# First-stage reordering in a two-layer diffusion trunk: raw products of four FFN column blocks, with the shift added later as a bias

## Chip, cores, metric

One Trainium2 chip, all 8 cores, every core running the same program on its own tokens. The metric is the device time in microseconds of the slowest core. "us" is microseconds throughout. Engines go by their names in the trace: PE is TensorE (matmuls), DVE VectorE, ACT ScalarE, POOL GpSimd, SP SyncE; PSUM is the memory into which PE writes its products (`ps` in the trace). Some executions are in a slower state: cores of one die (cores 0 to 3 or 4 to 7), or pairs of cores, show a lower granted TensorE clock (in one execution of head_only cores 0 to 3 had 0.811 to 0.819 and took 1687 to 1696 us, in another cores 2 to 5 had 0.968 to 0.971 and took 1455 to 1459; the other cores had 0.988 or more and took 1427 to 1432). Only fast executions enter the ratios. I also use "undisturbed cores": the mean span of all cores whose mean granted clock was 0.988 or more, over all executions of a kernel. That mean is steadier than a median.

## The reference, cut to what matters

```python
D_MODEL, D_FF, DEPTH = 1024, 2816, 2
def modulate(x, g, shift, scale):
    return rms_norm(x, g) * (1 + scale[:, None, :]) + shift[:, None, :]
def swiglu(h, w1, w2):
    gate, up = jnp.split(h @ w1, 2, axis=-1)
    return (jax.nn.silu(gate) * up) @ w2
# each layer: FFN 1, mixer, FFN 2; layer 0's mixer is convolution + attention, layer 1's pools
mod = jax.nn.silu(cvec) @ ada_w[l] + ada_b[l]            # 9 vectors of 1024 per layer
sh1, sc1, g1, sh2, sc2, g2, sh3, sc3, g3 = jnp.split(mod, 9, axis=-1)
x = x + 0.5 * g1 * swiglu(modulate(x, norm_g[l, 0], sh1, sc1), ffn_w1[l, 0], ffn_w2[l, 0])
# ... mixer with sh2, sc2, g2; second FFN with sh3, sc3, g3
```

The change uses a plain identity: with `r` the norm factor, `(x*r*scale + shift) @ W = (x*r*scale) @ W + shift @ W`. The second product does not depend on the token, so it is a bias per column.

## The kernel before

Tokens are split into three tiles per core: 512, 512 and 256 columns (`TILES`), held transposed, eight chunks of 128 features each. Operations are yielded by generators, and a scheduler places them on the engines in time order of a model, so the diff alone doesn't tell the final order. The first up-projection has 22 column blocks (`w1`), each 1 MB read as fp32 and stored as 512 KB of bf16. A modulation slot (`ada`) is as big: slots 0 to 3 of layer 0 hold the first shift, 4 to 7 the first scale; these eight are done on PE ("16 matmuls of 128x2" in the trace), all later ones as vector dots on DVE ("CUSTOM_DVE" in the trace, 4 per slot). All weights arrive through one queue of loads and one ring of 16 buffers:

```python
def seq():                                   # the order of loads
    a = list(w1(0, 0))
    for i in range(4):
        if i == 3:
            yield from a[0:2]
        yield from ada(0, 4 + i, 5 + i)      # scale
        yield from ada(0, i, i + 1)          # shift
    yield from a[2:6]
    self.pace = 0                            # from here loads are spaced by LOAD_GAPS
    yield from mix(a[6:], ada(0, 8, 24))
    yield from w2(0, 0)
    yield from ada(0, 24, 28)
    # ... mixer weights ...
    yield from mix(w1(0, 1), list(ada(0, 28, 36)) + list(ada(1, 0, 0)))
    yield from w2(0, 1)
    yield from ada(1, 0, 17)
    # ... layer 1 ...
yield from self.xtile(0, POOL)               # tile 0; tiles 1 and 2 are put in between:
for key, src, shape in seq():
    if key in (("ada", 0, 6), ("w1", 0, 0, 3)):
        yield from self.xtile(1 if key[0] == "ada" else 2, POOL)

def xload(self):                             # small tables and two row broadcasts, on another queue
    yield self.wait(("w", ("ada", 0, 3)))    # ... only after this slot has landed
    self.late = self.W[("ada", 0, 3)][1]
```

The norm of a tile makes squares by a plan (which engine squares each chunk, and whether PE sums it alone or it is first added up), then scales on DVE and adds the shift, mostly on ACT:

```python
A8 = [(ACT, False)] * 8                              # squares on ACT, added up on DVE
P8 = [(POOL, False)] * 6 + [(ACT, False)] * 2        # six squares on POOL, added up on POOL
Q8 = [(POOL, False)] * 6 + [(ACT, True)] * 2         # the two of ACT summed on PE
IN = [(ACT, True), (DVE, True)] * 4                  # every square summed on PE, in fp32
norms(1, 0, 0, [IN, IN, A8])                         # first FFN's norm, tiles 0, 1, 2
norms(2, 0, 1, [P8, P8, Q8], sh=(ACT, ACT, DVE))     # the norm before mixer 0
# in norm():
for c in range(8):
    yield self.wait(("mod", l, i, c // 2), 2)        # scale AND shift of this chunk
    yield self.stt(nv, xres[c], asc[c], r, ALU.mult, ALU.mult, ...)      # DVE
    # then hbuf = nv + shift, on ACT
```

## Time and profile before

Three runs took 1430.21 to 1431.3 us, median 1430.92. The profiled execution was a slow one, and its second die shows why it is not read:

The spans and clocks of the cores, kernel before (two of its lines):

```profile
core 0: 1427.0 us, clock 0.992
...
die 1 (median of its cores): 1442.5 us, clock 0.981
```

So I read core 0, of the undisturbed die. The table of stretches for it (stretch in us, then busy us and count of PE, weight loads, DVE, ACT, POOL; then the granted clock, the busy share of the DMA engines, and GB/s moved):

```profile
20.00:40.00 20.00, 11.41 (x80) 5.34 (x80) 6.67 (x15) 6.57 (x11) 2.84 (x6) 0.74 1.03 223
40.00:60.00 20.00, 15.15 (x76) 5.74 (x77) 9.21 (x17) 9.43 (x14) 1.10 (x3) 0.75 1.00 194
60.00:80.00 20.00, 20.00 (x94) 9.20 (x93) 9.29 (x18) 15.40 (x24) 0.00 (x0) 1.00 1.03 181
80.00:100.00 20.00, 20.00 (x128) 12.39 (x127) 16.00 (x30) 7.22 (x16) 0.53 (x1) 1.00 0.73 124
...
400.00:500.00 100.00, 96.53 (x1127) 50.73 (x1126) 55.16 (x135) 92.97 (x105) 20.56 (x23) 1.00 0.46 79
```

PE is full from about 57 us on, apart from small holes in the mixer and in attention. Before that it starves, while the DMA share is 1.0. The timeline of PE shows for what (start, duration, instruction and count; in brackets the idle time before it and what ended it; `sb_hbuf,sb_ring` is FFN work, `sb_scb` modulation, `sb_onesf` the sums of the norm):

```profile
22.52 0.58 PE L309 MATMUL ps<-sb_scb,sb_ring 128*128 128x2 bf16 x16 [3.22 <-DMA sb_ring<-adaw]
25.37 0.59 PE L309 MATMUL ps<-sb_scb,sb_ring 128*128 128x2 bf16 x16 [2.27 <-DMA sb_ring<-adaw]
28.82 8.52 PE L309 MATMUL ps<-sb_sq,sb_onesf 128*128 128x512 f32 x14 [2.86 <-ACT sb_sq L325]
...
45.40 6.70 PE L309 MATMUL ps<-sb_hbuf,sb_ring 128*128 128x512 bf16 x20 [1.24 <-ACT sb_hbuf L325]
...
56.71 14.78 PE L309 MATMUL ps<-sb_hbuf,sb_ring 128*128 128x512 bf16 x60 [1.68 <-ACT sb_hbuf L325]
```

A useful number for such a head is the *effective dense start*: the time at which PE would have had to start, without a pause, to be where it is. The first FFN's up-projection is 704 matmuls of 512 columns and 352 of 256, at the dense pace 704 x 0.2157 + 352 x 0.1092 = 190.3 us; it ended at 241.4 us, so this start is 51.1 us.

### The profile page before, as it was taken

What the parts mean: (1) busy time and instruction counts of PE and PEld (TensorE: products, weight loads), DVE (VectorE), ACT (ScalarE), POOL (GpSimd) and SP (SyncE); (2) the same over time, 40 slices, a digit from 0 to 9 for tenths busy, and PEclk for the clock granted to TensorE, in tenths of its full rate; (3) what the DMA queues carried; (4) which work ended last, traced back from release to release, by engine and by line L of the source; (5) the groups of instructions that cost most, each with busy time, mean ns of one, the idle gap of its engine ahead of it and who ended that gap; (6) DMA issues with size and microseconds to landing.
All of it is one profiled execution on the core that took longest, in us unless ns stands there. A gap on an engine that the chain in (4) does not pass through costs nothing.

```text
span 1443.6 us, 21515 instructions; the slowest of 8 cores (1423.7 to 1443.6 us)
## 1 busy us (share of the span) xinstructions
PE 1409.3 (98%) x8742; PEld 768.4 (53%) x8742; DVE 842.0 (58%) x1505; ACT 494.8 (34%) x824; POOL 207.1 (14%) x308
## 2 busy tenths in 40 slices
PE   5899999999999999999999999999999999999998
PEld 2355555457644554655544655555446646555446
DVE  2468872866656596342599977773575862222245
ACT  3441111035589956211123331111134771111112
POOL 3001111843312200110010011111110000000000
PEclk8899999999999999999999999999999999999999
DMA  9967779322555423663463377777861255550012
GB/s 201 190 110 123 125 121 172 70 34 39 93 90 88 75 39 65 101 118 59 74 105 58 58 122 127 121 125 119 131 106 30 44 88 89 94 95 16 0 59 89
DMA packets 42435, 132.24 MB, mean 92 GB/s; under 512 B 6240, under 2 KB 10080, under 8 KB 42336
## 3 DMA queue, kind: packets, MB, share of 16 engines
q0 software_dynamic: 34816, 122.52, 50.1%
q1 hardware_dynamic: 7520, 8.34, 1.8%
q8 instruction: 69, 1.13, 0.3%
q14 instruction: 30, 0.25, 0.1%
HBM read 241.55 MB, written 6.55 MB: 172 GB/s over the span
## 4 chain that ended last, share of the span: by engine, by line
PE 92%; POOL 2%; DVE 2%; ACT 2%; DMA 2%; issue 1%; DVEq 0%; ACTq 0%; POOLq 0%
PE ps L309 91%; DMA sb_xres<-xin 2%; DVE sb_nt L330 1%; POOL sb_ring L335 1%; POOL sb_sq L335 1%; ACT sb_sg L325 0%; POOL sb_acc L335 0%; POOL sb_areg L1306 0%; ACT sb_hbuf L325 0%; PE ps L318 0%; DVE sb_xres L330 0%; ACT sb_areg L325 0%; DVE sb_sq L688 0%; DVE sb_areg L330 0%; DVE sb_areg L335 0%
## 5 line engine op out<-in xcount | busy, mean ns | idle before, releaser
L309 PE MATMUL ps<-sb_hbuf,sb_ring 128*128 128x512 bf16 (+1 forms) x4512 | 842.9, 347 | 6.8 <-ACT sb_hbuf L325 3.6
L309 PEld LDWEIGHTS ps<-sb_hbuf,sb_ring 128*128 128x128 bf16 x4512 | 439.1, 99 | 380.4 <-issue 36.0
L309 PE MATMUL ps<-sb_areg,sb_ring 128*128 128x512 bf16 (+2 forms) x2480 | 428.0, 334 | 0.6 <-DVE sb_xres L330 0.6
L335 DVE TENSOR_TENSOR sb_areg<-ps,sb_sg 128x512 bf16<-128x512 f32 (+1 forms) x264 | 157.9, 602 | 327.6 <-PE ps L309 301.0
L325 ACT ACTIVATE sb_sg<-ps 128x512 f32<-128x512 f32 (+3 forms) x279 | 145.9, 527 | 544.5 <-PE ps L309 520.2
L309 PEld LDWEIGHTS ps<-sb_areg,sb_ring 128*128 128x128 bf16 x2480 | 229.3, 99 | 193.8 <-issue 19.7
L688 DVE CUSTOM_DVE_ANT_0 sb_sq<-sb_ring,sb_crow,sb_adab 128x1024 bf16<-128x1024 bf16 x128 | 167.4, 1308 | 22.7 <-DMA sb_ring<-adaw 22.1
L688 DVE CUSTOM_DVE_ANT_0 sb_ring<-sb_ring,sb_crow,sb_adab 128x1024 bf16<-128x1024 bf16 x128 | 167.6, 1309 | 2.4
L325 ACT ACTIVATE sb_sq<-sb_xres 128x512 f32<-128x512 f32 (+2 forms) x133 | 70.1, 534 | 267.4 <-DVE sb_xres L330 186.2
L330 DVE SCALAR_TENSOR_TENSOR sb_xres<-ps,sb_gsc,sb_xres 128x512 f32<-128x512 f32 (+2 forms) x160 | 98.3, 628 | 88.4 <-PE ps L309 87.4
L360 POOL DMA_DIRECT2D sb_ring<-w1t x88 | 47.2, 537 | 462.9 <-PE ps L309 397.9
L330 DVE SCALAR_TENSOR_TENSOR sb_nt<-sb_xres,sb_asc,sb_acc 128x512 f32<-128x512 f32 (+1 forms) x144 | 90.5, 664 | 12.8 <-ACT sb_acc L325 8.4
L325 ACT ACTIVATE sb_hbuf<-sb_nt,sb_modsb 128x512 bf16<-128x512 f32 (+1 forms) x136 | 84.9, 656 | 37.5 <-DVE sb_nt L330 37.1
L335 DVE TENSOR_TENSOR sb_acc<-sb_acc,sb_sq 128x512 f32<-128x512 f32 (+2 forms) x119 | 68.3, 574 | 26.6 <-ACT sb_sq L325 25.1
L360 POOL DMA_DIRECT2D sb_ring<-adaw x72 | 38.5, 539 | 302.9 <-PE ps L309 186.7
L325 ACT ACTIVATE sb_sg<-ps,sb_amask 128x1024 bf16<-128x1024 f32 x63 | 68.1, 1119 | 5.2 <-PE ps L309 4.9
L309 PE MATMUL ps<-sb_areg 128*128 128x65 bf16 (+3 forms) x600 | 61.1, 266 | 2.1 <-ACT sb_sg L325 1.8
L360 POOL DMA_DIRECT2D sb_ring<-w2t x44 | 23.3, 531 | 188.7 <-PE ps L309 175.0
L309 PEld LDWEIGHTS ps<-sb_areg 128*128 128x128 bf16 (+1 forms) x600 | 28.9, 96 | 38.1 <-issue 27.3
L309 PE MATMUL ps<-sb_ring,sb_hbuf 128*128 128x256 bf16 x320 | 38.1, 274 | 0.6 <-ACT sb_areg L325 0.3
L309 PE MATMUL ps<-sb_sq,sb_onesf 128*128 128x512 f32 (+2 forms) x44 | 24.2, 685 | 14.6 <-DVE sb_sq L335 11.0
L325 ACT ACTIVATE sb_areg<-ps,sb_amask 128x1024 bf16<-128x1024 f32 x33 | 36.3, 1116 | 4.0 <-PE ps L309 3.7
(74 smaller groups left out, 486.0 us busy)
## 6 DMA issues: line engine op xcount, KB each, us to landing
sb_ring<-w1t POOLq DMA_DIRECT2D x88, 512.0 KB, 5.1
sb_ring<-adaw POOLq DMA_DIRECT2D x72, 512.0 KB, 5.6
sb_ring<-w2t POOLq DMA_DIRECT2D x44, 512.0 KB, 5.2
sb_xres<-xin POOLq DMA_DIRECT2D x4, 1024.0 KB, 17.1
yo<-sb_xres SPq DMA_DIRECT2D x8, 512.0 KB, 3.0
sb_areg<-mp POOLq DMA_DIRECT2D x5, 512.0 KB, 8.2
sb_ring<-wcx POOLq DMA_DIRECT2D x4, 512.0 KB, 13.3
sb_ring<-wo POOLq DMA_DIRECT2D x4, 512.0 KB, 11.4
```

The costliest lines, as they stand in the source:

```text
L309: ins = e.matmul(m[0], lhsT=m[1], rhs=m[2], start=m[3], stop=m[4], **({"skip_group_check": True} if len(m) > 5 else {}))
L325: o = Op(ACT, lambda e: e.activation(out=out, in_=in_, func=func, **kw), reads, writes, cost)
L330: return Op(DVE, lambda e: e.scalar_tensor_tensor(out=out, in0=in0, scalar=scalar, in1=in1, op0=op0, op1=op1), reads, writes, 150.0 + 1.04 ...
L335: return Op(eng, lambda e: e.tensor_tensor(out=out, in0=in0, in1=in1, op=op), reads, writes, c)
L360: return Op(q, lambda e: e.dma_start(out=out, in_=in_), reads, writes, 600.0 if q == POOL else 450.0, True, nbytes, key)
L688: return Op(DVE, lambda e: e.tensor_tensor_reduce(out=prod, in0=w, in1=self.crow[:, v, :], scale=1.0, scalar=bias, op0=ALU.mult, op1=ALU.a ...
```

## The change

Intent: the last shift lands much later than the last scale could. So the four scale slots and four `w1` blocks are loaded before the four shift slots, and PE multiplies the scaled tokens of tiles 0 and 1 with those four blocks while the shifts are still on their way. The products are put aside in fp32 on chip. Later `shift @ W` is made for the four blocks (one column of PE output each), and the silu and the product take it as a bias. Three side changes come with it: the plans of the first norm (tile 1, the second tile, from `IN` to `A8`; tile 2, the third, from `A8` to `Q8`), the shift-adds of every other chunk of the second tile, which go from ACT to POOL, and a retuning of the gaps and the order of later loads and vector dots.

```diff
-ADA_GAP0, ADA_GAP = 600.0, 600.0
-LOAD_GAPS = (3900.0, 4400.0, 4000.0, 5500.0)
+ADA_GAPS = (((0, 22), 1000.0), ((0, 28), 600.0), ((0, 32), 600.0), ((1, 4), 1500.0), ((1, 13), 900.0), ((1, 26), 1500.0), ((1, 36), 800.0))
+NRAW = 4
+LOAD_GAPS = (3700.0, 4200.0, 4100.0, 5500.0)
 ... in seq():
-            for i in range(4):
-                if i == 3:
-                    yield from a[0:2]
-                yield from ada(0, 4 + i, 5 + i)
-                yield from ada(0, i, i + 1)
-            yield from a[2:6]
+            yield a[0]
+            yield from ada(0, 4, 5)
+            yield a[1]
+            yield from ada(0, 5, 8)
+            yield from a[2:NRAW]
+            yield from ada(0, 0, 4)
+            yield from a[NRAW:8]
             self.pace = 0
-            yield from mix(a[6:], ada(0, 8, 24))
+            yield from mix(a[8:], ada(0, 8, 22))
             yield from w2(0, 0)
-            yield from ada(0, 24, 28)
+            yield from ada(0, 22, 28)
 ... second FFN:
-            yield from mix(w1(0, 1), list(ada(0, 28, 36)) + list(ada(1, 0, 0)))
+            a = list(w1(0, 1))
+            yield from mix(a[0:6], ada(0, 28, 32))
+            yield from mix(a[6:], list(ada(0, 32, 36)) + list(ada(1, 0, 4)))
             yield from w2(0, 1)
-            yield from ada(1, 0, 17)
+            yield from ada(1, 4, 14)
 ... (layer 1: the same shift of slots, cut)
-            if key in (("ada", 0, 6), ("w1", 0, 0, 3)):
-                yield from self.xtile(1 if key[0] == "ada" else 2, POOL)
+            if key in (("w1", 0, 0, 1), ("w1", 0, 0, NRAW + 1)):
+                yield from self.xtile(1 if key[3] == 1 else 2, POOL)
 ... in norm(), tiles 0 and 1 of the first FFN:
+            for c in range(8):
+                yield self.wait(("scale", l, i, c // 2))
+                yield self.stt(hbuf[c], xres[c], asc[c], r, ALU.mult, ALU.mult, ...)
+                self.sigl(("h1", t))
+            yield self.wait(("raw", t), NRAW)      # then the usual loop, with shift
-                if sh == ACT:
+                if ver == 1 and t == 1 and c % 2:      # second tile, odd chunks: the shift is added on POOL
+                    yield Op(POOL, lambda e: e.tensor_scalar(out=hv, in0=nv, scalar1=b, ..., op0=ALU.add), ...)
+                elif sh == ACT:
 ... in ffn(): raw() multiplies, rawevac() puts aside and later finishes:
+                yield self.cp(vs2[0], vs[0], [bs[0]], [bs2[0]], ACT)     # PSUM -> fp32 in SBUF
+                yield self.cp(vs2[1], vs[1], [bs[1]], [bs2[1]])          # the same on DVE
+            yield self.wait(("bias", j))
+            yield self.act(sv, vs[0], AF.Silu, [bs[0], bb], [b], bias=self.bias[:, j, 0:1], scale=1.0)
+            yield self.stt(a[t][:, j, :], vs[1], self.bias[:, j, 1:2], sv, ALU.add, ALU.mult, ...)
 ... (shifts(): shift @ W, 16 one-column matmuls per block; cut)
-        norms(1, 0, 0, [IN, IN, A8])
+        norms(1, 0, 0, [IN, A8, Q8])
```

## The prediction

> **What bounds the kernel now.** Median 1430.92 us. The profiled execution fell in the slow state, so I read core 0 of the undisturbed die (span 1427.0 us, clock 0.992). PE is busy 97% (engine shares). The table of stretches puts 23.4 of its 36 idle us before 60 us; later there are about 12 (3.5 in attention at 400 to 500 us, 5.9 at the tail). Only the head has something to give.
>
> In the head (PE timeline) dense work starts late. By 71.33 us PE has done 96 FFN matmuls of 128x512; at the dense pace (85 in 18.51 us, 0.218 us each) those are 20.9 us: an effective dense start at 50.4 us. Before it PE waits for modulation weights, ordered scale, shift, scale, shift. The DMA share is about 1.0 from 10 to 60 us; the waits show landings at 22.5, 25.4 and 28.1 us: some 2.75 us per 1 MB read. The last modulation slot is MB number 14. PE also does 32 fp32 sum-of-squares matmuls, 8.2 us or more for each of the first two tiles.
>
> **What the change moves.** The four scale slots come before the four shift slots, with four w1 blocks among them. At 2.75 us per MB my estimate of landings is: first w1 block 17, first scale 19, second x tile 25, second w1 28, other scales 31, 34, 36, third and fourth w1 39 and 42, shifts 44 to 53, fifth w1 55. For tiles 0 and 1, four blocks (128 matmuls, 27.9 us dense) need scales only. The build order puts 26 of them ahead of the last scale.
>
> Added: 64 one-column shift matmuls, about 0.55 us per 16 (cost of the existing modulation groups), 2.2 us of PE; eight evacuations to fp32 on ACT and eight on DVE, 0.6 to 0.7 us each; sixteen second scalings on DVE, 0.75 us each, 12 us; some shift-adds on POOL. DVE, about a third busy at 20 to 60 us, becomes nearly full. Removed from PE: fourteen fp32 passes of the second tile, about 7 us; they stood in DMA time.
>
> **On the critical path.** After the last scale (36 us plus 0.9) PE has 102 raw matmuls (22.2 us), 2.2 us of shift-weight groups, 2.2 us of shift products and some 2 us from reduced clock: it ends near 65 us with 128 matmuls done, an effective dense start near 37 us. [...]granted 0.50 from 44 to 48 us and 1.00 from 50. Gain 13.5 us, less about 1 us for more sums of the third tile on PE. The retuned load and vector gaps should move little.
>
> **Predicted: 1418 us, 1410 to 1426 (8 in 10).** Faster by over 2% 0.01, within 2% 0.97, slower by over 2% 0.02.
>
> **What would show it.** First dense FFN run starts at 30 to 37 us, not 56; PE idle before 60 us drops from 23 to about 10 us; DMA share still 1.0 to 60 us; shift products at about 60 us with no wait over 1 us; everything from the second FFN on runs the same, 13 us earlier.
>
> **What would make it wrong.** DVE, nearly full at 35 to 65 us, holding bank evacuations, so PE waits: 3 to 8 us. Half clock through the sparse phase: 2 to 4. The gain given back in mixer 0, where vector-made modulation arrives no earlier (the chain of waits passes through adaw and DVE at 237 to 253 us): up to 12.

The sum: 36.9 + 22.2 + 2.2 + 2.2 + 2 = 65.5 us, taken as 65; that less 128 x 0.218 = 27.9 for the 128 matmuls is the dense start near 37; 50.4 less this is the gain of 13.5, less 1 it is 12.5, from 1430.9 to 1418 us. The 2 us of reduced clock are the author's estimate, as much as 4 us at the granted 0.50 of 44 to 48 us would lose.

## The result

The changed kernel is correct. Four runs: 1431.13, 1433.39, 1433.72 and 1506.48 us (the last slow), median 1433.56; the kernel before beside it has a median of 1431.11. The ratio of fast runs is 1.0012, with an interval from 0.9993 to 1.0032: the same. (A ratio here is the mean time of one kernel's fast runs over that of the other's in the same rounds, so not quite the ratio of the medians quoted.) The predicted range, 1410 to 1426, does not hold it.

The table of stretches of core 0, changed kernel, against that of before:

```profile
20.00:40.00 20.00, 11.67 (x72) 4.38 (x72) 12.54 (x26) 7.16 (x12) 1.61 (x3) 0.66 1.03 204
40.00:60.00 20.00, 20.00 (x151) 9.94 (x150) 12.75 (x27) 5.86 (x10) 2.05 (x4) 1.00 1.03 180
60.00:80.00 20.00, 17.57 (x145) 8.65 (x144) 15.15 (x25) 13.64 (x22) 11.25 (x13) 0.91 1.01 198
80.00:100.00 20.00, 17.77 (x83) 8.32 (x82) 14.19 (x25) 12.82 (x21) 6.09 (x4) 1.00 0.74 127
...
400.00:500.00 100.00, 95.05 (x1102) 50.26 (x1101) 61.37 (x144) 91.33 (x104) 22.55 (x24) 1.00 0.45 77
```

40 to 60 us is now what was hoped for: 20.00 busy us for 15.15. But 60 to 100 us, full before, now has 4.7 idle us and a clock of 0.91. The timeline of PE shows both:

```profile
28.99 1.89 PE L312 MATMUL ps<-sb_hbuf,sb_ring 128*128 128x512 bf16 x4 [4.13 <-DMA sb_ring<-w1t]
...
41.90 9.22 PE L312 MATMUL ps<-sb_hbuf,sb_ring 128*128 128x512 bf16 x42
...
66.25 4.48 PE L312 MATMUL ps<-sb_hbuf,sb_ring 128*128 128x512 bf16 x20
73.16 5.31 PE L312 MATMUL ps<-sb_hbuf,sb_ring 128*128 128x512 bf16 x16 [2.43 <-DMA sb_ring<-w1t]
...
88.91 11.38 PE L312 MATMUL ps<-sb_hbuf,sb_ring 128*128 128x512 bf16 x52 [2.23 <-ACT sb_crow L328]
```

At 66.25 us PE has done 124 of the 128 raw matmuls: 66.25 - 124 x 0.2157 = 39.5, an effective dense start 11.6 us earlier than before. At 88.91 us it has done 192 up-projection matmuls of 512 columns: 88.91 - 192 x 0.2157 = 47.5. So 8 us of the lead are lost in 23 us on this core: 2.43 of waiting for the sixth `w1` block, then 5.31 - 16 x 0.2157 = 1.9 because the clock had gone down (granted 0.50 from 75 to 77 us, by the table of stretches), 1.6 for fp32 sums of the third tile (0.6 of it also before), and 2.23 of a last wait. The timeline puts the last wait down to ACT (`sb_crow`, the silu of the two rows that the vector dots need), but that is only the latest count of a semaphore that PE also looks at. What PE needs is in the program: the matmuls at 88.91 us are the second tile's first ones with the shift, and they read all eight chunks of that tile. A semaphore instruction of PE just before them, which the views do not print, waits from 82.65 to 88.85 us and is released by POOL. These are POOL's shift-adds, and a scaling of DVE between them (the third and fourth columns are engine and line):

```profile
81.36 1.99 POOL L863 TENSOR_SCALAR sb_hbuf<-sb_nt,sb_modsb 128x512 bf16<-128x512 f32 x1 [4.44 <-DVE sb_nt L333]
84.37 1.93 POOL L863 TENSOR_SCALAR sb_hbuf<-sb_nt,sb_modsb 128x512 bf16<-128x512 f32 x1 [1.02 <-DVE sb_nt L333]
...
86.40 0.75 DVE L333 SCALAR_TENSOR_TENSOR sb_nt<-sb_xres,sb_asc,sb_acc 128x512 f32<-128x512 f32 x1 [1.53 <-POOL sb_hbuf L863]
...
87.25 1.56 POOL L863 TENSOR_SCALAR sb_hbuf<-sb_nt,sb_modsb 128x512 bf16<-128x512 f32 x1 [0.95 <-DVE sb_nt L333]
```

DVE scales a chunk into one of two buffers (`sb_nt`), POOL adds the shift and frees the buffer, and each waits for the other in turn. The last add ends at 88.81 us, and PE goes on at 88.91.

Core 0 is not typical, so the same marks were taken on all eight cores. The wait for the sixth block is 2.43 us on core 0, at most 1.32 on the others. On the other seven PE waits at 77 to 79 us for the third tile's squares, added up on POOL (`sb_acc`): 1.24 to 3.10 us. Core 2:

```profile
78.27 0.67 PE L312 MATMUL ps<-sb_acc,sb_onesf 128*128 128x256 f32 x2 [3.10 <-POOL sb_acc L338]
```

The wait for the last shift-add is 2.23 us on core 0, 0.94 on three cores and not seen on four. On average the effective dense start is 40.4 us where the shift products end and 46.5 at the first down-projection matmul: 6.1 us are lost, 8.0 on core 0.

To follow the rest, these are marks in the trace, as means of the undisturbed cores of the profiled execution:

| mark (us) | before | after | lead of after |
|---|---|---|---|
| first down-projection matmul of FFN 1 | 240.9 | 236.8 | 4.1 |
| first q/k/v matmul of mixer 0 | 296.0 | 296.1 | -0.1 |
| first up-projection matmul of FFN 2 | 532.0 | 535.5 | -3.5 |
| end | 1425.6 | 1429.0 | -3.4 |

The column of the kernel before rests on four cores of one execution: before_norm2_act below, which has the same first FFN, puts the first mark at 242.4, so this lead of 4.1 us may be up to 1.5 us larger. The lead is lost three times over: 6 us (mean of the cores) at 66 to 95 us, 4 us in mixer 0, and 3.4 more in attention. After that both kernels run alike. The loss in mixer 0 is one hole. PE at 284 to 300 us, before:

```profile
286.40 1.12 PE L309 MATMUL ps<-sb_acc,sb_onesf 128*128 128x512 f32 x2 [1.39 <-DVE sb_acc L335]
287.37 9.66 PE L309 MATMUL ps<-sb_areg,sb_ring 128*128 128x512 bf16 x44
297.14 2.79 PE L309 MATMUL ps<-sb_ring,sb_hbuf 128*128 128x256 bf16 x24
```

and after:

```profile
284.73 1.17 PE L312 MATMUL ps<-sb_acc,sb_onesf 128*128 128x512 f32 x2 [4.00 <-DVE sb_acc L338]
285.70 11.35 PE L312 MATMUL ps<-sb_areg,sb_ring 128*128 128x512 bf16 x44
296.88 2.78 PE L312 MATMUL ps<-sb_ring,sb_hbuf 128*128 128x256 bf16 x24
```

PE arrives early, waits 4.00 us for the sum of squares of the mixer's norm, and then runs the next 44 matmuls at a lower clock (11.35 us for 9.66; granted 0.61 from 286 to 290 us, 1.00 in the kernel before). What DVE does just before, in the changed kernel (the dots come in twos; the other lines are additions of squares and the last evictions of the down-projection into `sb_xres`):

```profile
279.40 0.69 DVE L338 TENSOR_TENSOR sb_acc<-sb_acc,sb_sq 128x512 f32<-128x512 f32 x1 [4.17 <-ACT sb_sq L328]
280.01 1.28 DVE L699 CUSTOM_DVE_ANT_0 sb_sq<-sb_ring,sb_crow,sb_adab 128x1024 bf16<-128x1024 bf16 x1
...
281.33 1.28 DVE L699 CUSTOM_DVE_ANT_0 sb_ring<-sb_ring,sb_crow,sb_adab 128x1024 bf16<-128x1024 bf16 x1
...
282.54 0.75 DVE L333 SCALAR_TENSOR_TENSOR sb_xres<-ps,sb_gsc,sb_xres 128x512 f32<-128x512 f32 x1
283.99 0.69 DVE L338 TENSOR_TENSOR sb_acc<-sb_acc,sb_sq 128x512 f32<-128x512 f32 x1 [0.69 <-ACT sb_sq L328]
```

Two dots of modulation slot 27 stand in front of the eviction at 282.54, and the sum that PE waits for comes after it. They stand there because DVE had itself waited (4.17 us at 279.40) at the end of a chain of squares and additions that POOL ran from 248.9 to 278.6 us. In that chain POOL also makes six products for the rotary tables (`sb_ring<-sb_ring,sb_qkg`), 10.7 us together; no run moves them.

In attention, PE's waits from 300 to 560 us (us in total, times, longest), two of the lines before:

```profile
PE ps L309 <- ACT sb_sg L325: 1.8, 3, 0.8
...
PE ps L309 <- DVE sb_areg L335: 0.5, 1, 0.5
```

and after:

```profile
PE ps L312 <- DVE sb_areg L338: 3.9, 4, 1.5
PE ps L312 <- ACT sb_sg L328: 2.5, 5, 0.8
```

The wait for DVE grew from 0.5 to 3.9 us. Between 400 and 545 us DVE runs 24 dots in the changed kernel and 16 before (counted in the timeline), so the retuned order of loads is suspected.

### The profile page after: what moved, and what is told of

It reads as the page before. It is cut to its first block, busy times and chain, and to the rows that moved or that the text cites. A ratio compares the mean times of both kernels' runs of the same rounds, so it can differ in the third digit from the quotient of the medians.

```text
span 1431.6 us, 21667 instructions; the slowest of 8 cores (1426.8 to 1431.6 us)
## 1 busy us (share of the span) xinstructions
PE 1390.4 (97%) x8796; PEld 763.6 (53%) x8796; DVE 856.4 (60%) x1533; ACT 492.2 (34%) x822; POOL 225.9 (16%) x323
## 4 chain that ended last, share of the span: by engine, by line
PE 90%; POOL 3%; DVE 3%; ACT 2%; DMA 2%; issue 1%; another core or an unknown queue 0%; DVEq 0%; ACTq 0%; POOLq 0%
PE ps L312 90%; DMA sb_ring<-w1t 2%; ACT sb_sg L328 1%; POOL sb_sq L338 1%; POOL sb_ring L338 1%; DVE sb_sq L699 1%; ACT sb_areg L328 0%; POOL sb_acc L338 0%; DVE sb_xres L333 0%; POOL sb_areg L1398 0%; PE ps L321 0%; DVE sb_nt L333 0%; DVE sb_areg L338 0%; DVE sb_areg L333 0%; DVE sb_acc L338 0%
## 5 line engine op out<-in xcount | busy, mean ns | idle before, releaser
L312 PE MATMUL ps<-sb_areg,sb_ring 128*128 128x512 bf16 (+2 forms) x2480 | 422.9, 332 | 0.0
L338 DVE TENSOR_TENSOR sb_areg<-ps,sb_sg 128x512 bf16<-128x512 f32 (+1 forms) x256 | 152.6, 599 | 309.7 <-PE ps L312 290.2
L328 ACT ACTIVATE sb_sg<-ps 128x512 f32<-128x512 f32 (+3 forms) x270 | 140.3, 523 | 530.7 <-PE ps L312 507.4
L328 ACT ACTIVATE sb_sg<-ps,sb_amask 128x1024 bf16<-128x1024 f32 x64 | 69.5, 1119 | 8.4 <-PE ps L312 7.9
L328 ACT ACTIVATE sb_areg<-ps 128x128 f32<-128x128 f32 (+5 forms) x58 | 26.1, 478 | 46.3 <-PE ps L312 30.9
## 6 DMA issues: line engine op xcount, KB each, us to landing
sb_ring<-wcx POOLq DMA_DIRECT2D x4, 512.0 KB, 11.6
sb_ring<-wo POOLq DMA_DIRECT2D x4, 512.0 KB, 10.2
```

The costliest lines, as they stand in the source:

```text
L312: ins = e.matmul(m[0], lhsT=m[1], rhs=m[2], start=m[3], stop=m[4], **({"skip_group_check": True} if len(m) > 5 else {}))
L328: o = Op(ACT, lambda e: e.activation(out=out, in_=in_, func=func, **kw), reads, writes, cost)
L338: return Op(eng, lambda e: e.tensor_tensor(out=out, in0=in0, in1=in1, op=op), reads, writes, c)
```

## The experiments

The theory after the result: the reordering of the head works as meant up to 66 us; loads and the third tile's norm behind it take most of the lead; the mixer's norm takes the rest; the retuning costs some 3 us in attention. The rivals: the head itself gains nothing (raw evacuations on DVE, low clock); the retuning is what is wrong with the kernel; or the mixer bounds the time whatever the head does. All fifteen kernels below gave correct results. Chips differ by up to 2.5 us in the undisturbed cores of the unchanged kernel, so each kernel is compared with the kernel before on the same chip. "Undisturbed" gives the mean span of undisturbed cores minus that of the kernel before on that chip.

| kernel | first down | q/k/v | FFN 2 up | undisturbed | ratio of fast runs (95%) |
|---|---|---|---|---|---|
| after_again | 236.9 | 296.5 | 535.6 | +1.8 | 1.0005 (0.9988 to 1.0022) |
| head_only | 237.2 | 299.1 | 535.4 | +2.5 | none (one fast run) |
| retune_only | 242.8 | 296.1 | 533.3 | 0.0 | 0.9997 (0.9981 to 1.0012) |
| late_extras | 240.1 | 293.4 | 530.9 | -2.0 | 1.0165 (see there) |
| norm2_act | 236.3 | 289.6 | 528.5 | -4.2 | 0.9963 (0.9945 to 0.9981) |
| slot27_late | 236.3 | 289.6 | 532.0 | -2.5 | 0.9985 (0.9962 to 1.0007) |
| before_norm2_act | 242.4 | 296.5 | 532.7 | -1.5 | 0.9980 (0.9958 to 1.0003) |
| late_t2act | 231.9 | 285.3 | 523.9 | -10.2 | 0.9922 (0.9903 to 0.9942) |
| late_t2act_norm2 | 231.5 | 284.8 | 523.6 | -9.9 | 0.9924 (0.9904 to 0.9943) |
| att_loads | 237.5 | 297.0 | 533.9 | +4.6 | 1.0038 (1.0014 to 1.0062) |
| late_t2act_att | 231.7 | 285.1 | 522.4 | -6.2 | 0.9953 (0.9933 to 0.9973) |
| before_late | 243.0 | 296.2 | 532.2 | -1.7 | 0.9980 (0.9963 to 0.9998) |
| t2act | 234.1 | 295.8 | 538.1 | +3.5 | 1.0035 (1.0018 to 1.0051) |
| after_l1 | 237.9 | 297.2 | 534.3 | -1.0 | 0.9995 (0.9980 to 1.0010) |
| late_t2act_l1 | 232.2 | 285.6 | 522.0 | -11.7 | 0.9914 (0.9897 to 0.9931) |

### The changed kernel once more

No edit.

> The changed kernel itself, for comparison on the same chip. Every theory: undisturbed cores 2 us (1 to 3) longer than those of the kernel before; first down matmul near 236.8 us, first q/k/v matmul near 296.1, first matmul of the second FFN's up-projection near 535.5. The stretch from q/k/v to the second up-projection takes 239.4 us. If these marks move by more than 1 us on another chip, differences of 1 to 2 us between other runs mean nothing.

Measured: +1.8 us on undisturbed cores, marks 236.9, 296.5 and 535.6, a stretch of 239.1 us from q/k/v to the second up-projection. The marks come back within 0.4 us on another chip, so differences of 2 us between the stages of two kernels mean something.

### The two halves of the change: head_only and retune_only

```diff
 head_only, against after: gaps and later load order of the kernel before
-ADA_GAPS = (((0, 22), 1000.0), ((0, 28), 600.0), ... )
-LOAD_GAPS = (3700.0, 4200.0, 4100.0, 5500.0)
+ADA_GAPS = (((1, 36), 600.0),)
+LOAD_GAPS = (3900.0, 4400.0, 4000.0, 5500.0)
 (and the splits of ada slots 22/24, 28 to 36, layer 1 as before)
 retune_only, against before: the same lines the other way round, head untouched
```

> The changed kernel with the retuning (load gaps, vector gaps, split of the modulation loads) undone; only the head is new. Theory A (the head gains about 4 us by the start of the first down-projection, and in-order queues of the next stage hand it back whatever the gaps are): 1428 to 1434 us, first down matmul at 236 to 238 us on the undisturbed cores, first q/k/v matmul at 296 to 298. Theory B (the retuning costs what the head gained): 1426 us or less, and the start of the second FFN's up-projection at 528 to 531 us instead of 533 to 538.

Measured: five of six runs were slow, so there is no ratio; the only fast one took 1433.41 us, and the undisturbed cores are at +2.5, like the whole change. The first down-projection comes at 237.2, so the head's gain of about 4 us belongs to the head. But q/k/v come at 299.1: here PE waits for down-projection weights at about 245 us (3.7 to 7.5 us over the eight cores, in the view of waits), because the old gap of loads, 3900, and the two modulation slots more in front of `w2` bring it too late for a first FFN that ends earlier (the run puts both back and doesn't separate them). The attention stretch is 236.3 us, as before the change.

> The kernel before with the retuned gaps and split alone, old head. Theory A: within 3 us of before, 1428 to 1434 us, as the gaps matter little by themselves. Theory B (the retuning costs 5 us or more in the attention stage through more vector-made modulation there): 1435 to 1438 us.

Measured: 0.0 us, ratio 0.9997. The retuning alone is neutral in total. So it is not "what is wrong with the kernel", but it is no gain either; its part seems to be to bring `w2` early enough for the new head.

### The loads behind the raw products: late_extras

```diff
 def xload(self):
-    yield self.wait(("w", ("ada", 0, 3)))
-    self.late = self.W[("ada", 0, 3)][1]
+    yield self.wait(("w", ("w1", 0, 0, NRAW + 3)))
+    self.late = self.W[("w1", 0, 0, NRAW + 3)][1]
-            if key in (("w1", 0, 0, 1), ("w1", 0, 0, NRAW + 1)):
+            if key in (("w1", 0, 0, 1), ("w1", 0, 0, NRAW + 4)):
```

Why this was tried: in the changed kernel the sixth block stands behind the third x tile (1 MB), and from 56 us a second queue starts to compete. The sync engine's timeline, changed kernel, shows its first issue, two row broadcasts of 512 KB:

```profile
56.63 1.01 SPq L363 DMA_DIRECT2D sb_ring<-crow  x2
```

and the view of DMA from 60 to 76 us shows what the two queues moved (packets, MB, share of the 16 engines):

```profile
q0 software_dynamic: 619, 2.25, 76.5%
q1 hardware_dynamic: 530, 1.06, 24.3%
```

A quarter of the engines' time goes to tables that nobody needs yet, just when PE runs out of weights.

> The changed kernel with the third x tile three w1 blocks later and the small tables and rows for the modulation held until the eighth w1 block has landed. Theory S (the head gains only 3.7 us because the sixth w1 block comes at the pace of the loads: 1 MB of third tile and about 1.3 MB of small loads stand before it): no PE wait on w1 after 66 us (2.4 us before), first down matmul 3 to 6 us earlier than in the changed kernel, at 231 to 234 us. Rival (the wait is ACT's queue, not the loads): first down matmul within 1 us of the changed kernel's. Total: 1427 to 1434 us if the next stage hands it back, 1428 or less if not.

Measured: the wait for the sixth block is gone, but the head is no better (240.1), because a new wait has come. PE in this kernel, core 0:

```profile
65.58 18.07 PE L312 MATMUL ps<-sb_hbuf,sb_ring 128*128 128x512 bf16 x82
89.65 1.19 PE L312 MATMUL ps<-sb_acc,sb_onesf 128*128 128x256 f32 x2 [5.99 <-POOL sb_acc L338]
```

82 matmuls run through without a hole, and then PE waits 5.99 us (5.99 to 6.01 on all eight cores) for the third tile's squares on POOL. They start at 74.2 us where they started at 61.7, as the tile lands late, and now share POOL with the second tile's shift-adds. The expectation was wrong about the size: it did not see this. The times of this kernel are not comparable: in five of six executions one or two pairs of cores took about 1450 us, at a mean clock of 0.971, and in the sixth a whole die took over 1650; that is what the 1.0165 shows. The other cores were at -2.0. More on that in the last section.

### The third tile's norm: late_t2act and t2act

late_t2act is late_extras and one more line; t2act is that line alone in the changed kernel:

```diff
-        norms(1, 0, 0, [IN, A8, Q8])
+        norms(1, 0, 0, [IN, A8, A8])
```

> The changed kernel with the late third tile and small loads, and the third tile's squares on ACT as they were before the change (POOL's chain held PE for 6.0 us in the run with late loads alone). Theory S (w1 supply at the head is worth what PE lost there: 2.4 us wait, 1.9 us at reduced clock, 2.2 us behind ACT): no PE wait over 1.5 us between 66 and 120 us, first down matmul at 231 to 234 us, 3 to 6 us earlier than the changed kernel's 236.7. Rival: another wait takes its place and it stays at 235 us or later. The next stage's wait may grow; total 1420 to 1428 us on undisturbed cores.

Measured: ratio 0.9922, undisturbed cores at -10.2. PE's timeline, core 0:

```profile
66.38 22.64 PE L312 MATMUL ps<-sb_hbuf,sb_ring 128*128 128x512 bf16 x98
88.86 0.59 PE L312 MATMUL ps<-sb_acc,sb_onesf 128*128 128x256 f32 x2
89.51 12.68 PE L312 MATMUL ps<-sb_hbuf,sb_ring 128*128 128x512 bf16 x57
```

No hole is left (no wait of PE over 0.6 us between 66 and 120 us on any core), and the first down-projection comes at 231.9, 9.0 us before that of the kernel before: the head's gain is there once the two waits are away. Also q/k/v come at 285.3, so the mixer no longer takes the lead back. In this kernel modulation slot 27 is started at 259 us and not at 270, so no dot stands in front of the last eviction, and PE has no wait there.

> The changed kernel with only the third tile's first squares on ScalarE instead of GpSimd; its loads stay where they are. Theory: the wait for the sixth weight block at 70 us stays and bounds the first FFN, so the first down matmul comes within 1.5 us of 236.9 us and the undisturbed cores within 1.5 us of the changed kernel's. Rival: the third tile's norm was the real hold and the late loads added nothing: first down matmul at 232 to 234 us.

Measured: first down-projection at 234.1, that is 2.8 us earlier than after_again, though the wait for the sixth block stays:

```profile
73.27 17.38 PE L312 MATMUL ps<-sb_hbuf,sb_ring 128*128 128x512 bf16 x71 [2.63 <-DMA sb_ring<-w1t]
```

The theory (within 1.5 us of 236.9) was wrong, and the rival's range, 232 to 234, was just missed. So the third tile's plan is worth 2.8 us at this mark by itself, and the late loads 2.2 us on top of it (231.9), while the late loads alone are a loss of 3 (240.1): the late loads need the plan. The plan does two things. No squares of the third tile are left on POOL for PE to wait for. And it changes the scheduler's order: building both programs shows that 80 matmuls of the first tile, and not 64, now stand in front of the second tile's first ones, 3.5 us more of work. On core 0 the last shift-add (86.70 to 88.27 us) then ends before PE would have to stop. Which of the two is worth how much isn't separated. All of t2act's gain is gone at q/k/v (a wait of 4.0 us, as in the changed kernel; its slot 27 still starts at 270 us) and it ends 3.5 us behind the kernel before, with 242.3 us for the attention stretch. Why that stretch is longer still is open.

### The norm before mixer 0: norm2_act, slot27_late, before_norm2_act, late_t2act_norm2

```diff
 norm2_act (against after), before_norm2_act (against before), late_t2act_norm2 (against late_t2act)
-        norms(2, 0, 1, [P8, P8, Q8], sh=(ACT, ACT, DVE))
+        norms(2, 0, 1, [A8, P8, Q8], sh=(ACT, ACT, DVE))
 slot27_late (against after)
-            yield from ada(0, 22, 28)
+            yield from ada(0, 22, 27)
 ... and ada(0, 27, 28) after the load of ("wb", 1)
```

The first moves the squares of the tile that PE waits for from POOL to ACT. The second leaves POOL alone and takes away the two dots.

> The changed kernel with the squares of the second norm's first tile on ACT (idle there for 40 us) and their sums on DVE, instead of POOL. Theory N (POOL's chain of squares and sums, 249 to 278 us, holds DVE's queue, so PE waits 4.0 us and then runs at reduced clock): that wait falls under 1 us, first q/k/v matmul 4 to 6 us earlier, at 291 to 293 us, total 1427 to 1430 us. Rival (the evictions behind modulation dots on DVE hold it, whoever squares): wait stays 3 us or more, total within 1.5 us of the changed kernel.

> The changed kernel with one modulation load (the fourth slot of the third shift) moved behind the mixer's weights, so that its two dots no longer stand on DVE between the last evictions of the first down tile. Theory D (the chain of squares on POOL is as long as before, 30 us, but those two dots of 1.3 us hold the last eviction, and the 4.0 us wait cools the clock): the wait before the first norm sum falls from 4.0 to about 1.4 us, no cold stretch after it, first q/k/v matmul 3 to 5 us earlier, at about 292 us, undisturbed cores at 1424 to 1426 us. Rival (POOL alone): wait stays 3 us or more, first q/k/v within 1.5 us of the changed kernel's 296 us.

Measured: norm2_act has q/k/v at 289.6 and is at -4.2 us, ratio 0.9963. slot27_late has q/k/v at 289.6, 6.5 us earlier than the changed kernel (3 to 5 were expected). Here is its PE:

```profile
261.71 19.80 PE L312 MATMUL ps<-sb_areg,sb_ring 128*128 128x512 bf16 x89
281.35 1.02 PE L312 MATMUL ps<-sb_acc,sb_onesf 128*128 128x512 f32 x2
282.20 9.66 PE L312 MATMUL ps<-sb_areg,sb_ring 128*128 128x512 bf16 x43
```

The wait is gone, and with it the clock's fall (9.66 us again). So either of two cures is enough: the dots are the last straw, the chain on POOL puts DVE where the dots meet it. slot27_late gives 3 us back in attention, where the slot now lies, and ends at -2.5.

Part of POOL's slowness may be DVE's doing; no run tests it alone, and what the two would share is not shown. In the trace of the changed kernel a 128x512 square on POOL takes 1.95 to 2.02 us while dots run, and 1.04 us at 275.8 us when DVE is idle; a dot takes 2.05 to 2.30 us at 270 to 275 us and 1.28 us at 280 us, when POOL does no arithmetic. But not every dot beside a square is slower: the one at 252.95 us took 1.28 us too.

> The kernel before with the same move of the first tile's squares from POOL to ACT. If the stage behind the first FFN was bound by that chain before the change too, it gains about the 2 us that PE waited there (1.4 and 0.5 us) and no more: undisturbed cores at 1424 to 1425 us instead of 1426.3, so that the changed kernel with this move (1422.1) is ahead of it by about the head's 3 to 4 us less what attention loses. If it gains nothing, 1426 to 1427; if it gains as much as the changed kernel did (6.5 us), 1420, and the head's gain would be worth nothing.

Measured: -1.5 us, q/k/v at 296.5. The same cure is worth 1.5 us before the change and about 6 after it (from +1.8 to -4.2). Before the change there was only a small wait there (1.39 us). So the mixer's norm is not a fault from which every kernel would gain as much when it is mended: it became a hold of 4 us because PE came earlier.

> Both repairs together: the head's loads and third-tile squares as in late_t2act, and the second norm's first tile on ACT. If head and mixer losses are separate and add: first down matmul 231 to 234 us, first q/k/v matmul 53 us later, 284 to 287, undisturbed cores at 1416 to 1419 us (1422.1 with the norm alone). If what the head gains is still handed back later: 1421 us or more.

Measured: -9.9 us, as without it. Where no wait is left, taking its cause away gains nothing.

### Are the late loads good without the change: before_late

```diff
 (against before)
-        yield self.wait(("w", ("ada", 0, 3)))
-        self.late = self.W[("ada", 0, 3)][1]
+        yield self.wait(("w", ("w1", 0, 0, 5)))
+        self.late = self.W[("w1", 0, 0, 5)][1]
-            if key in (("ada", 0, 6), ("w1", 0, 0, 3)):
+            if key in (("ada", 0, 6), ("w1", 0, 0, 6)):
```

> The kernel before, with its old first stage, and only the repair of the loads: third x tile after two more blocks of weights, small loads held until the block before has landed. Theory: before the change the first up-projection is held by the mixer's modulation and the norm, not by these loads, so the first down matmul stays within 1.5 us of 240.9 and the time within 0.2%. Rival: the repair is worth its 3 to 5 us whatever the head; then the first down matmul comes at 236 to 238 and the gain of the repaired version is not owed to the change.

Measured: first down-projection at 243.0 (expected within 1.5 us of 240.9, so a narrow miss on the slow side), undisturbed cores -1.7, ratio 0.9980. The rival, 236 to 238, is out. At this mark the old head gains nothing from late loads (before_norm2_act, with the old head and the old loads, has 242.4). In total it is 1.7 us faster, with an interval that just excludes 1. So at most some 2 of the 10 to 12 us of the repaired kernels could be owed to the repair alone; the rest is owed to the change with its repair.

### The attention stage: att_loads, late_t2act_att, after_l1, late_t2act_l1

```diff
 att_loads (against after), late_t2act_att (against late_t2act)
-            yield from mix(a[0:6], ada(0, 28, 32))
-            yield from mix(a[6:], list(ada(0, 32, 36)) + list(ada(1, 0, 4)))
+            yield from mix(a, ada(0, 28, 36))
             yield from w2(0, 1)
-            yield from ada(1, 4, 14)
+            yield from ada(1, 0, 14)
 after_l1 (against after), late_t2act_l1 (against late_t2act): everything from FFN 2 on as before
-ADA_GAPS = (((0, 22), 1000.0), ((0, 28), 600.0), ((0, 32), 600.0), ((1, 4), 1500.0), ... )
-LOAD_GAPS = (3700.0, 4200.0, 4100.0, 5500.0)
+ADA_GAPS = (((0, 22), 1000.0), ((1, 36), 600.0))
+LOAD_GAPS = (3700.0, 4400.0, 4000.0, 5500.0)
 (and the load order of FFN 2 and of layer 1 as before)
```

> The changed kernel with only the order of loads of the second up-projection and second down-projection put back as before, so that fewer modulation slots (and their vector dots) fall into the attention stage. Theory: those dots hold the vector engine's queue there (24 dots between 400 and 545 us against 16 before) and the tensor engine waits 3.9 us for it, so the stretch from q/k/v to the second up-projection takes 236 to 237.5 us in place of 239.4, and the undisturbed cores end 2 to 3 us earlier, level with the kernel before. Rival: the retuning of the loads is neutral there and the stretch stays at 239 or more; then the attention stage's loss comes from the phase in which it starts.

Measured: the stretch is 236.9 us, as the theory had it, with only 16 dots between 400 and 545 us. But the kernel ends at +4.6. Half of the expectation failed: after the second FFN's up-projection it loses 5.6 us that the changed kernel does not lose (707.5 us from the second FFN's first down-projection matmul to the end, 701.9 in after_again). PE's waits from 990 to 1160 us, core 0:

```profile
PE ps L312 <- DMA sb_ring<-w2t: 2.8, 1, 2.8
PE ps L312 <- ACT sb_hbuf L328: 2.0, 1, 2.0
```

In the changed kernel this window has no wait of PE at all. As I read it, with four slots fewer done early and the wide gaps of 900 to 1500 kept, layer 1's modulation and the weights behind it come too late. The retuned order and the retuned gaps are one package.

> The best version so far (third tile and small loads late, third tile's first norm split over two ScalarE plans) with the same order of loads in the second up-projection. Theory: q/k/v start at 285.3 as in that run, the stretch to the second up-projection falls from 238.6 to 236 to 237.5, undisturbed cores near 1416.5 in place of 1418.5. Rival: the stretch stays at 238 or more and the end does not move.

Measured: the same: 237.3 us in the stretch, then a loss of the same size (707.8 us to the end), -6.2 in all.

> The changed kernel with order, gaps of vector dots and gaps of loads all as before from the second up-projection on; the first stage keeps its retuning. Theory: the attention stage's loss and the later loss in att_loads both come from a mixed retuning, so q/k/v to the second up-projection takes 236 to 237.5 us in place of 239.1, and from the second FFN's down-projection to the end 702 us as in both kernels, not the 707.5 of att_loads; undisturbed cores level with the kernel before, within 1 us. Rival: 238.5 us or more in attention, or over 704 us after it, which would mean the changed first stage needs the changed second one.

Measured: 237.1 us in the stretch, 702.3 us from the second FFN's first down-projection matmul to the end (702.0 before; 707.5 in att_loads), undisturbed cores at -1.0. All three as the theory said. So some 2 us of the attention stage's loss of 3.4 (239.4 against 236.0 before) are owed to the second half of the retuning, and come off when the whole package goes. They are not owed to it alone: retune_only, with the old head, has 27 dots of DVE between 400 and 545 us and still takes only 237.2. Why the retuning costs more behind the new head is open.

> The best version with the second layer's loads and gaps put back as before. Theory: q/k/v at 285.1, the second up-projection at 521.5 to 522.5, 702 us from the second down-projection to the end, undisturbed cores 1416 to 1417, about 11 us under the kernel before, ratio 0.990 to 0.992. Rival: 1418.5 or more as in the best version without it: ratio 0.992 to 0.994.

Measured: q/k/v at 285.6, FFN 2 at 522.0, undisturbed cores at 1416.6 us, -11.7. The median is 1420.57 us against 1432.75, ratio 0.9914 (0.9897 to 0.9931). This is the best version: about 12 us faster than the kernel before and 13 than the changed one, by four edits, none of which touches the arithmetic of the change.

## Why the prediction was right or wrong

**Right: what bounds the kernel.** The head starved for modulation loads, and the raw products fill it. The first dense run starts at 41.9 us (said: 30 to 37, so 5 us late), shift products run at 62 to 66 us without a wait over 1 us (said: about 60), the DMA share is 1.0 to 60 us, and at 66 us the effective dense start is 39.5 on core 0, 40.4 on the mean of the cores. The prediction said PE would end "near 65 us with 128 matmuls done, an effective dense start near 37 us". That step held within 2.5 us on core 0 and 3.4 on the mean. Part of the error is in the loads: the estimate was 2.75 us per MB read, while the table of stretches gives 170 GB/s written from 28 to 56 us, so that the 524,288 bytes of a slot took 3.1 us (worked out from that figure).

**Wrong: the step from there to the time.** The text goes straight from "an effective dense start near 37 us" to "Gain 13.5 us, less about 1 us for more sums of the third tile on PE". This takes it that a PE that is early at 66 us stays early. It assumed four things to be free, and each cost time:

1. *The loads after the fourth block.* The estimate of landings ends with "fifth w1 55". It never asked for the sixth, which stands behind the third x tile and shares the engines with 1.06 MB of tables. It came at 73 us: on core 0 2.43 us of wait and 1.9 of low clock, on the other cores 0 to 1.32 us of wait.
2. *The norms of the second and third tile.* The third tile's was costed as PE work, "about 1 us", which is right for PE (1.0 us more of fp32 sums). What it really cost was PE's wait for POOL's squares: 1.24 to 3.10 us on seven cores of the changed kernel, and 6.0 in late_extras, where the first wait was gone and the tile came later still. Of the second tile's the prediction lists "some shift-adds on POOL" and gives them no place on the path: PE waited 2.23 us for the last of them on core 0, 0.94 on three other cores. Points 1 and 2, with the low clock, took 6.1 us in the changed kernel (mean of the cores; 8.0 on core 0); late_t2act, without these waits, has the first down-projection 4.9 us earlier and 9.0 before that of the kernel before.
3. *Mixer 0.* The prediction did name it: "The gain given back in mixer 0, where vector-made modulation arrives no earlier". The place was right, and two dots of that modulation did stand in the way. But they held DVE's queue, not their own user: PE waited for a sum of squares that POOL's chain and these dots delayed. It took the remaining 4 us. norm2_act and slot27_late each take the hold away.
4. *The retuning.* "The retuned load and vector gaps should move little." In total that holds for the old head (retune_only, 0.0). Behind the new head it cost some 2 us in attention: 239.1 us for the stretch against 236.9 and 237.1 in att_loads and after_l1.

The sum, from the marks: of 12.5 us predicted, 3 were never there (40.4 for 37, at 66 us), 6 went from there to 95 us, 4 in mixer 0, and attention added a loss of 3.4. That makes a loss of 4 us; measured were 1429.0 on undisturbed cores against 1425.6, a loss of 3.4, where about 1413 was expected.

**Feared, and did not come.** "DVE, nearly full at 35 to 65 us, holding bank evacuations": DVE was busy 12.75 of 20 us, and no wait of PE names an evacuation in that time. The low clock was expected in the head and was there (0.66 granted at 20 to 40 us, 1.00 from 40 to 60); it cost time later too, after the new waits (0.50 from 75 to 77 us, 0.61 from 286 to 290), where I had not looked for any.

**Open.** Why t2act's attention stretch is 242.3 us. Why the retuning costs attention more behind the new head than behind the old. Why slot 27's dots start at 259 us with late loads and at 270 without: the loads and the dots are paced by a scheduler's model, and I did not take that apart.

## What to carry to other kernels

When a stage is made to start earlier, list what comes *after* it in the same queues (next loads, small tables, the next tile's norm, the next stage's slow helper engine) and give each its own time of arrival; a lead is only worth what the latest of these allows. Two repairs can depend on each other: one that shows nothing alone (late loads: a loss of 3 us) can be part of what works (9 us with the second line); when a new wait shows up in place of the old, mend that too before judging. Retuned gaps and orders of loads belong to the kernel that they were tuned for: undo or keep them as a package, stage by stage, and read each stage's stretch and not the total. Look at more than one core before naming a wait: the wait for the sixth block, 2.43 us on core 0, was at most 1.32 on the others. And where the profile names a releaser that the waiting work doesn't read, look for another.

## What the traces show of the clock, the table loads and the second queue

- In the fast execution of the changed kernel that was profiled, all eight cores have a granted clock of 1.00 from 290 to 1424 us (mean of that stretch), with PE busy 1119 to 1126 of these 1134 us. In late_extras' profiled execution cores 4 and 5 have means of 0.971 and 0.972 over the whole span: core 4 was at 0.81 from 100 us and came back to 1.00 at 260 us, with PE fully busy (the columns are those of the table of stretches; core 0 was at 1.00 from 100 us on):

```profile
100.00:180.00 80.00, 80.00 (x411) 44.43 (x409) 51.01 (x88) 14.40 (x31) 9.33 (x18) 0.81 0.70 115
180.00:260.00 80.00, 80.00 (x370) 40.09 (x369) 49.62 (x89) 12.02 (x23) 10.05 (x19) 0.81 0.77 125
260.00:300.00 40.00, 40.00 (x195) 18.89 (x194) 36.15 (x50) 3.06 (x5) 27.01 (x18) 1.00 0.35 66
```

  It cost the pair about 27 us (1450 against 1424). It began at the restart after an idle time of PE that all eight cores had together (6.0 us on each); in head_only's profiled execution cores 2 to 5 went to 0.81 after a common wait of 3.7 to 7.5 us, and came back at about 415 us. Whether the common pause and restart set it off is not shown: only one execution of each is traced, and in both the other cores (four in head_only, six in late_extras) had the same pause and a mean clock of 0.990 or more. Some slow runs of other kernels had all four cores of a die at a mean clock of 0.81 to 0.91 (spans of 1545 to 1703 us).
- In the changed kernel, core 0, 2.43 us of idle (at 70.7 us) were followed by 16 matmuls in 5.31 us where 3.45 is dense (16 x 0.2157), while 2.23 us of idle (at 86.7 us) cost the next 52 nothing (11.38 us). On five of the eight cores idle times of 2.22 to 2.86 us were followed by one stretch of 3.41 us at a granted clock of 0.50; on core 2, 3.10 us of idle were followed by none. So in this trace the length of the idle time alone doesn't decide.
- A load of an activation table on ACT takes 1.28 us (at 83.18 and 85.95 us in the changed kernel), and no idle time beside it shows there: at 85.95 us the load starts 0.02 us after the activation before it ended, and the next activation starts 0.01 us after the load.
- In the changed kernel the small loads on the second queue (1.06 MB) had 24.3% of the DMA engines' time from 60 to 76 us and the large ones on the first 76.5%, just in front of a block that PE waited for.
